# A recurrent branch and an attention without GpSimd arithmetic: products on VectorE, a value kept in DRAM, a first tap on ScalarE

## The chip, the cores and the metric

The kernel runs on one core of a Trainium2 chip. The engines of the core that matter here are TensorE (PE in the profile: matrix products), VectorE (DVE), ScalarE (ACT), GpSimd (POOL) and SyncE (SP, which here only issues DMAs). Each engine works through its own queue of instructions in a fixed order and waits on semaphores for the others. The metric is the time of one execution on the device in microseconds. Lower is better.

## What is computed

Two blocks in sequence on a tensor of 1024 positions by 1024 channels, all in float32. The change touches the recurrent branch of the first block, the tail of that block's MLP, and the row sums of the second block's attention. Of the reference:

```python
# first block
z = jnp.einsum("bsd,de->bse", rms_norm(x, g_mix), w_in) + b_in
va, ga, xb, gb, sa, sb = jnp.split(z, cuts, axis=-1)
u = causal_depthwise_conv(va * sigmoid(ga), conv_a_w, conv_a_b)      # 31 taps, 1024 channels
y_a = silu(layer_norm(u, ln_g, ln_b)) @ w_a_out
v = causal_depthwise_conv(xb, conv_b_w, conv_b_b)                    # 4 taps, 1536 channels
# rg_lru, 16 heads of 96 channels:
r = sigmoid(block_diag_linear(v, w_a, b_a)); i = sigmoid(block_diag_linear(v, w_x, b_x))
log_a = -8.0 * r * softplus(-lam); a = exp(log_a)
mult = sqrt(-expm1(2.0 * log_a)), with 1.0 at the first position
h = scan over positions of  h = a * h + mult * i * v
y_b = (h * gelu(gb)) @ w_b_out
x = x + (sigmoid(sa) * y_a + sigmoid(sb) * y_b) @ w_o
x = x + square(relu(rms_norm(x, g_mlp) @ w_1)) @ w_2
x = rms_norm(x, g_final)
# second block (mLSTM, pooling and memory attention branches)
s = einsum(q, k) * exp(dmat - m_t)        # causal, per chunk in the reference
h = (... + s @ v) / max(abs(... + sum(s, axis=-1)), exp(-m_t))
```

## The kernel before, in words

Every tensor lies with 128 channels in the partitions and positions along the free axis, in two halves of 512 positions (`hf`). A float32 matrix product is made as three products of split values (a high part made by a ScalarE copy, a low part made by a VectorE subtraction). A tile of 128 channels by 512 positions takes 24 matmuls (`ct`, `mm3`, L124 and L127). A weight block of 128x1024 arrives by DMA (L106, two buffers `wst`), gets its high part on ACT (L108) and its low part on DVE (L110).

The Tile scheduler places the instructions of all these code pieces into the engines' queues by priority at build time. After that the order of each queue is fixed.

The input projection of the first block, `mixer_in`, runs from about 20 to 690 us in four rounds `r` of `branch_b`. In a round:

- `branch_b_in` runs three times, for three blocks of 128 channels: two `ct` tiles, ACT moves them out to page `x6` with a bias (L376), POOL makes the first of the four short taps into page `x7` (L381, 128x1024), DVE adds the three others (L383), SP stores rows 96 to 127 to `v_d` (L385), and ACT and DVE split the result into `vh` and `vl`.
- a filler: in rounds 0 to 2 two more channel blocks of the long convolution, whose 31 taps are DVE instructions of 128x512 (L358) with low priority, spread over the following work; in round 3 tiles of the two sigmoid gates (`sig_chunk`, L471).
- four heads `n`. In each, ACT moves four gate tiles out of PSUM with a sigmoid (L416, into buffers `a`), then makes two exponentials (L421, two more buffers `a`), two tanh (L425) and two squares (L428, buffers `c`); DVE combines them (L429); ACT takes two roots (L432); DVE writes the start value (L433). For n < 3 PE makes the gelu input, two `ct` tiles, and ACT makes gelu (L442 for 96 rows into buffer `b`, L443 for the other 32 into `gl_d`). Then per half: POOL rebuilds the conv result r = vh + vl into a buffer `c` (L451, n < 3; the fourth head's r is `v_d`), POOL makes i * r (L454), DVE multiplies by the root (L455), DVE scans (L456), POOL multiplies by gelu (L458), SP stores the result to `p` (L460, L463).

There are six buffers `a`, and a head takes six. So the gates and exponentials of a head go into buffers that the head before has to have finished with. The last readers there are L455, L456 and, for the buffers of the two input gates, POOL's L458. There are five buffers `c`, of which `gl_d` holds two for the round. PSUM has four buffers `pa` (gates) and four `pm` (`ct`).

Elsewhere POOL makes half of the sums of squares at the end of the MLP (`square_sum`, L155, 14 additions of 128x512), and in the second block's attention (`mlstm_attn`) the causal select L789 and the running row sum L798 (40 additions). In the attention DVE makes the decay argument (L785), ACT its exponential (L786), DVE the product with the scores (L791), ACT and DVE split that (L131, L132), and PE's L800 and L801 use the split.

The lines of the last steps of a head, in before:

```python
                if n < 3:
                    G.tensor_tensor(r, src[hf][0].bitcast(F32), src[hf][1].bitcast(F32), ALU.add)
                else:
                    r = v_d[hf][rows, :]
                G.tensor_tensor(i_, i_, r, ALU.mult)
                V.tensor_tensor(i_, i_, m[hf][rows, :], ALU.mult)
                V.tensor_tensor_scan(i_, a[hf][rows, :], i_, 0.0 if prev is None else prev[:, HALF - 1:HALF], ALU.mult, ALU.add)
                prev = i_
                G.tensor_tensor(gt, gt, i_, ALU.mult)
```

## Time and profile before

| | us |
|---|---|
| median of 3 runs (2460.03 to 2460.41) | 2460.33 |
| the profiled execution | 2459.31 |
| its span, first to last instruction | 2457.6 |
| PE busy | 2366.8 (96%) |
| DVE busy | 1521.3 (62%) |
| ACT busy | 869.6 (35%) |
| POOL busy | 323.1 (13%) |
| mean granted clock of PE, share of full | 0.984 |

PE is busy nearly all the time, and the shares of the others are averages over stages that differ: DVE is at nine tenths or more in most slices of the first 740 us, and at three to six tenths in most of the rest. What the time depends on must be read by stretches: the row of 40 slices shows where an engine is full, the windows view gives the busy time, the instruction counts and PE's clock in a stretch, the view of waits tells which instruction ended PE's idle times, and the timeline of an engine shows what stood in its queue.

### The profile page before, as it was taken

How to read it: one execution, taken by the hardware profiler on the slowest of the kernel's cores; microseconds unless marked ns; L12 is line 12 of the kernel's file. 1: busy time of each engine (PE TensorE's matmuls, PEld its weight loads, DVE VectorE, ACT ScalarE, POOL GpSimd, SP SyncE). 2: the span in 40 equal slices, each digit the busy share in tenths (PEclk: the TensorE clock that was granted, in tenths of full speed). 3: DMA queues.
4: the chain of work that ended last, by engine and by line, in shares of the span. 5: the costliest groups of instructions: out<-in, count | busy, mean ns of one | idle time of the engine just before them, and what ended most of it. 6: DMA issues, size and time to landing. Idle time of an engine off the chain costs nothing.

```text
span 2457.6 us, 27022 instructions
## 1 busy us (share of the span) xinstructions
PE 2366.8 (96%) x10656; PEld 1946.1 (79%) x10656; DVE 1521.3 (62%) x2115; ACT 869.6 (35%) x1358; POOL 323.1 (13%) x198
## 2 busy tenths in 40 slices
PE   8996989989999999999999999999899999999998
PEld 6875867868878888888888888888688787777777
DVE  8998999698473424563333333434846557874766
ACT  6344254353652302342122112213524344442432
POOL 0127142153400000000000000001200002220110
PEclk9998999989999999999999999999999999999999
DMA  4111212113233422321211111121331111213331
GB/s 150 58 50 46 67 48 92 56 45 91 83 124 110 160 85 82 99 67 43 61 35 60 43 52 52 35 66 38 103 103 54 55 61 50 72 60 117 115 100 69
DMA packets 71104, 181.64 MB, mean 74 GB/s; under 512 B 8496, under 2 KB 11056, under 8 KB 70976
## 3 DMA queue, kind: packets, MB, share of 16 engines
q1 hardware_dynamic: 70976, 179.92, 23.4%
q8 instruction: 83, 1.36, 0.2%
q14 instruction: 45, 0.37, 0.0%
HBM read 148.92 MB, written 29.39 MB: 73 GB/s over the span
## 4 chain that ended last, share of the span: by engine, by line
PE 65%; DVE 22%; issue 5%; ACT 4%; POOL 3%; DMA 1%; SPq 0%; DVEq 0%; ACTq 0%; POOLq 0%
PE pm L124 41%; PE pm L127 20%; DVE e L358 8%; DVE wl L110 2%; DVE x L383 1%; POOL x L381 1%; DVE a L456 1%; DVE a L132 1%; PE pa L124 1%; DVE roll L723 1%; ACT wh L108 1%; PE pm L119 1%; DVE a L791 1%; DVE a L455 1%; DMA ld<-y 1%
## 5 line engine op out<-in xcount | busy, mean ns | idle before, releaser
L124 PE MATMUL pm<-acth,wl 128*128 128x512 f32 (+1 forms) x2480 | 968.0, 391 | 26.3 <-ACT c L443 13.2
L124 PE MATMUL pm<-actl,wh 128*128 128x512 f32 (+1 forms) x2480 | 966.6, 391 | 0.0
L127 PE MATMUL pm<-acth,wh 128*128 128x512 f32 (+1 forms) x2480 | 619.8, 387 | 0.0
L124 PEld LDWEIGHTS pm<-acth,wl 128*128 128x128 f32 x2480 | 471.7, 190 | 124.8 <-ACT c L443 14.5
L124 PEld LDWEIGHTS pm<-actl,wh 128*128 128x128 f32 x2480 | 471.6, 190 | 96.3 <-issue 0.7
L127 PEld LDWEIGHTS pm<-acth,wh 128*128 128x128 f32 x2480 | 461.4, 188 | 94.3 <-issue 1.2
L108 ACT ACTIVATE wh<-wst 128x1024 fp32r<-128x1024 f32 x209 | 219.9, 1055 | 544.9 <-PE pm L127 501.7
L110 DVE TENSOR_TENSOR wl<-wst,wh 128x1024 fp32r<-128x1024 f32 x209 | 257.7, 1235 | 94.7 <-ACT wh L108 94.4
L124 PE MATMUL pm<-e,wl 128*128 128x512 f32 x592 | 230.4, 389 | 0.0
L124 PE MATMUL pm<-e,wh 128*128 128x512 f32 x592 | 230.3, 389 | 0.0
L646 DVE TENSOR_TENSOR x<-pm,x 128x512 f32<-128x512 f32 x128 | 88.4, 691 | 180.1 <-PE pm L127 180.1
L155 POOL TENSOR_TENSOR row<-row,c 128x512 f32<-128x512 f32 x14 | 22.4, 1598 | 1057.9 <-ACT c L152 1057.5
L127 PE MATMUL pm<-e,wh 128*128 128x512 f32 x592 | 158.1, 389 | 0.0
L636 DVE TENSOR_TENSOR b<-b 128x512 f32<-128x512 f32 x64 | 44.3, 692 | 178.0 <-ACT b L634 178.0
L358 DVE SCALAR_TENSOR_TENSOR e<-roll,pv,e 128x507 f32<-128x507 f32 (+13 forms) x174 | 151.7, 927 | 0.0
L124 PEld LDWEIGHTS pm<-e,wl 128*128 128x128 f32 x592 | 111.1, 188 | 23.4 <-DVE wl L110 0.4
L124 PEld LDWEIGHTS pm<-e,wh 128*128 128x128 f32 x592 | 111.1, 188 | 23.1
L127 PEld LDWEIGHTS pm<-e,wh 128*128 128x128 f32 x592 | 111.1, 188 | 23.1
L634 ACT ACTIVATE b<-pm 128x512 f32<-128x512 f32 x64 | 38.3, 598 | 204.0 <-PE pm L127 203.2
L458 POOL TENSOR_TENSOR b<-b,a 96x512 f32<-96x512 f32 x24 | 73.7, 3090 | 76.9 <-DVE a L456 55.9
L798 POOL TENSOR_TENSOR a<-a,a 128x256 f32<-128x256 f32 (+2 forms) x40 | 59.0, 1474 | 102.5 <-DVE a L791 100.9
L789 POOL TENSOR_SCALAR_AFFINE_SELECT a<-a 128x128 f32<-128x128 f32 (+1 forms) x32 | 17.2, 537 | 408.9 <-ACT a L786 408.9
(315 smaller groups left out, 2557.7 us busy)
## 6 DMA issues: line engine op xcount, KB each, us to landing
wst<-in_w_in SPq DMA_DIRECT2D x89, 512.0 KB, 3.6
wst<-in_w SPq DMA_DIRECT2D x64, 512.0 KB, 3.5
sig<-b SPq DMA_DIRECT2D x32, 256.0 KB, 2.5
ld<-sig SPq DMA_DIRECT2D x32, 256.0 KB, 2.7
a<-p SPq DMA_DIRECT2D x24, 256.0 KB, 4.1
wst<-in_w_b_out SPq DMA_DIRECT2D x12, 512.0 KB, 4.3
y<-b SPq DMA_DIRECT2D x24, 256.0 KB, 2.0
ld<-y SPq DMA_DIRECT2D x24, 256.0 KB, 2.6
```

What stands on the lines that cost most here:

```text
L108: nc.scalar.activation(h, st, AF.Copy)
L110: nc.vector.tensor_tensor(l, st, h.bitcast(F32), ALU.subtract)
L119: self.nc.tensor.matmul(ps, a, b, start=i == 0, stop=i == n - 1)
L124: self.nc.tensor.matmul(ps, a, b, start=i == 0, stop=i == n - 1)
L127: self.nc.tensor.matmul(ps, aH, bH, start=i == 0, stop=i == n - 1)
L132: self.nc.vector.tensor_tensor(L, srcap, H.bitcast(F32), ALU.subtract)
L358: ops.append(lambda k=k: V.scalar_tensor_tensor(out[:, k:], x[:, :HALF - k], taps[k], out[:, k:], ALU.mult, ALU.add))
L458: G.tensor_tensor(gt, gt, i_, ALU.mult)
L634: A.activation(t, ps, AF.Relu)
L636: V.tensor_tensor(t2, t, t, ALU.mult)
L646: V.tensor_tensor(x, ps, x, ALU.add)
L798: G.tensor_tensor(acc[:, n0:], acc[:, n0:], e[:, n0:], ALU.add)
```

## The change

The four parts of the change:

1. `branch_b_in`: the first short tap L381 (12 instructions of 128x1024) goes from POOL to ACT, as an activation with scale and bias. Rows 0 to 95 of the conv result are also stored to a DRAM tensor `v` (24 stores of 96x512).
2. `branch_b`: r is no longer rebuilt on POOL; 24 DMAs load it from `v` into a buffer `c`, on SP's queue. The product i * r (32 instructions) and the product with gelu (32) go from POOL to DVE.
3. `mlp`: the 14 additions of L155 go from POOL to DVE.
4. `mlstm_attn`: the 40 additions of the row sum go from POOL to DVE.

POOL keeps the causal select and a few instructions at the end. After the change a new line stands in `branch_b_in` at L386, so that L416 becomes L417, L421 L422, L428 L429, L429 L430, L432 L433 and L433 L434. The load of r is L453, the product i * r L456, the product with the root L457, the scan L458, the product with gelu L460, its store L462; in the attention L785 becomes L787, L791 L793, L798 L800.

```diff
--- before.py
+++ after.py
@@ -378,11 +378,12 @@
 
         def wt(s):
             return self.vec("conv_b_w", c * 4 + 3 - s)
-        nc.gpsimd.tensor_scalar(v, xb, wt(0), self.vec("conv_b_b", c), ALU.mult, ALU.add)
+        nc.scalar.activation(v, xb, AF.Identity, scale=wt(0), bias=self.vec("conv_b_b", c))
         for s in range(1, 4):
             V.scalar_tensor_tensor(v[:, s:], xb[:, :S - s], wt(s), v[:, s:], ALU.mult, ALU.add)
         for hf in range(2):
             nc.sync.dma_start(v_d[hf][32 * j:32 * j + 32, :], v[HEAD:P, hf * HALF:(hf + 1) * HALF])
+            nc.sync.dma_start(self.v_dram[c][hf], v[:HEAD, hf * HALF:(hf + 1) * HALF])
         vh = self.page(f"x{j}", F32R)
         vl = self.page(f"x{3 + j}", F32R)
         self.split(v, vh, vl)
@@ -446,16 +447,17 @@
                 gl = gl_d
             prev = None
             for hf in range(2):
-                r, i_, gt = (self.tmp('c')[rows, :] if n < 3 else None), gate[2 * hf + 1][rows, :], gl[hf][rows, :]
+                i_, gt = gate[2 * hf + 1][rows, :], gl[hf][rows, :]
                 if n < 3:
-                    G.tensor_tensor(r, src[hf][0].bitcast(F32), src[hf][1].bitcast(F32), ALU.add)
+                    r = self.tmp("c")[rows, :]
+                    nc.sync.dma_start(r, self.v_dram[3 * g + n][hf])
                 else:
                     r = v_d[hf][rows, :]
-                G.tensor_tensor(i_, i_, r, ALU.mult)
+                V.tensor_tensor(i_, i_, r, ALU.mult)
                 V.tensor_tensor(i_, i_, m[hf][rows, :], ALU.mult)
                 V.tensor_tensor_scan(i_, a[hf][rows, :], i_, 0.0 if prev is None else prev[:, HALF - 1:HALF], ALU.mult, ALU.add)
                 prev = i_
-                G.tensor_tensor(gt, gt, i_, ALU.mult)
+                V.tensor_tensor(gt, gt, i_, ALU.mult)
                 if n < 3:
                     nc.sync.dma_start(self.p_dram[3 * g + n][hf][0:HEAD, :], gt)
                 else:
@@ -646,7 +648,7 @@
                         V.tensor_tensor(x, ps, x, ALU.add)
                     if e == 7:
                         acc1 = self.square_sum(acc1, x)
-                        acc2 = self.square_sum(acc2, x, self.vec("g_final", c), nc.gpsimd)
+                        acc2 = self.square_sum(acc2, x, self.vec("g_final", c))
                 if e == 7:
                     V.scalar_tensor_tensor(acc2, acc1, EPS, acc2, ALU.mult, ALU.add)
                     rs = self.rsqrt(self.spread(acc2, self.mean_d), EPS * EPS)
@@ -795,7 +797,7 @@
                 if acc is None:
                     acc = e
                 else:
-                    G.tensor_tensor(acc[:, n0:], acc[:, n0:], e[:, n0:], ALU.add)
+                    V.tensor_tensor(acc[:, n0:], acc[:, n0:], e[:, n0:], ALU.add)
                 vH, vL = v(h, j)
                 M(num[:, n0:], vL, pH[:, n0:], start=j == 0, stop=False)
                 M(num[:, n0:], vH, pL[:, n0:], start=False, stop=False)
@@ -1051,6 +1053,7 @@
             def dt(n, i, shape):
                 return dram.tile(list(shape), F32, tag=f"{n}{i}", name=f"{n}{i}")
             self.p_dram = [[dt("p", 2 * c + hf, (P, HALF)) for hf in range(2)] for c in range(12)]
+            self.v_dram = [[dt("v", 2 * c + hf, (HEAD, HALF)) for hf in range(2)] for c in range(12)]
             self.sig_dram = [[dt("sig", 2 * c + hf, (P, HALF)) for hf in range(2)] for c in range(16)]
             self.y_dram = [[dt("y", 2 * c + hf, (P, HALF)) for hf in range(2)] for c in range(12)]
             self.x_dram = [[dt("xd", 2 * c + hf, (P, HALF)) for hf in range(2)] for c in range(8)]
```

**DVE's queue, round 0, the second head.** Before, from the head's two L429 on. The names are those of the program with running numbers: `a` a gate buffer, `c` a buffer of r or of a square, `e` and `roll` outputs and inputs of the long convolution.

```order
L429 SCALAR_TENSOR_TENSOR a_1607<-c_1633,a_1607 96x512
L429 SCALAR_TENSOR_TENSOR a_1619<-c_1636,a_1619 96x512
L358 SCALAR_TENSOR_TENSOR e_124_868<-roll_398,tap_sum,e_124_868 128x510
L358 SCALAR_TENSOR_TENSOR e_181_1422<-e_155_1133,pv,e_181_1422 128x511
L358 SCALAR_TENSOR_TENSOR e_180_1370<-e_154_1132,pv,e_180_1370 128x511
L433 MEMSET a_1607 96x1
L358 SCALAR_TENSOR_TENSOR e_123_816<-roll_329,tap_sum,e_123_816 128x509
L455 TENSOR_TENSOR a_1613<-a_1613,a_1607 96x512
L455 TENSOR_TENSOR a_1625<-a_1625,a_1619 96x512
L456 SCALAR_TENSOR_TENSOR a_1613<-a_1627,a_1613 96x512
L358 SCALAR_TENSOR_TENSOR e_124_868<-roll_398,tap_sum,e_124_868 128x509
L456 SCALAR_TENSOR_TENSOR a_1625<-a_1629,a_1613,a_1625 96x512
```

After, from the same place (L430 is what was L429):

```order
L430 SCALAR_TENSOR_TENSOR a_1637<-c_1663,a_1637 96x512
L430 SCALAR_TENSOR_TENSOR a_1649<-c_1666,a_1649 96x512
L110 TENSOR_TENSOR wl_1984<-wst_1980,wh_1982 128x1024
L456 TENSOR_TENSOR a_1643<-a_1643,c_1734 96x512
L434 MEMSET a_1637 96x1
L358 SCALAR_TENSOR_TENSOR e_124_892<-roll_422,tap_sum,e_124_892 128x510
L457 TENSOR_TENSOR a_1643<-a_1643,a_1637 96x512
L456 TENSOR_TENSOR a_1655<-a_1655,c_1741 96x512
L458 SCALAR_TENSOR_TENSOR a_1643<-a_1657,a_1643 96x512
L457 TENSOR_TENSOR a_1655<-a_1655,a_1649 96x512
L460 TENSOR_TENSOR b_1703<-b_1703,a_1643 96x512
L458 SCALAR_TENSOR_TENSOR a_1655<-a_1659,a_1643,a_1655 96x512
```

The two L456 and the first L460 now stand between the two L430 and the second scan, together with a weight's L110; of the five L358 that stood in this piece one is left there, the others are further back. The first product, which needs a loaded `c`, is the fourth row.

**SP's queue, the same place.** `wst` is a weight block, `p` the stored result, `v` the new DRAM tensor. Before:

```order
L106 DMA wst_1950<-in_w_in 128x1024
L460 DMA p_99<-b_1558 96x512
L106 DMA wst_2020<-in_w_in 128x1024
L460 DMA p_100<-b_1586 96x512
L460 DMA p_101<-b_1673 96x512
L460 DMA p_102<-b_1701 96x512
```

After:

```order
L106 DMA wst_1980<-in_w_in 128x1024
L453 DMA c_1619<-v_123 96x512
L453 DMA c_1626<-v_124 96x512
L106 DMA wst_2052<-in_w_in 128x1024
L462 DMA p_99<-b_1588 96x512
L462 DMA p_100<-b_1616 96x512
L453 DMA c_1734<-v_125 96x512
L453 DMA c_1741<-v_126 96x512
L106 DMA wst_2124<-in_w_in 128x1024
```

Each of these heads now has two loads of r ahead of a weight load and of two stores of `p`; the second load of a head writes the buffer `c` that the head's first L430 has read.

**DVE's queue, the end of the MLP, second half.** `row` are the two running sums of squares, L658 (after: L660) the scaling of the residual with the last norm, `wl` the low part of a weight of the second block. Before:

```order
L658 SCALAR_TENSOR_TENSOR x_1024_6992<-x_1024_6992,pv,row_11715 128x512
L110 TENSOR_TENSOR wl_12294<-wst_12290,wh_12292 128x1024
L155 TENSOR_TENSOR row_11958<-row_11958,c_12036 128x512
L658 SCALAR_TENSOR_TENSOR x_1028_7023<-x_1028_7023,pv,row_11715 128x512
L110 TENSOR_TENSOR wl_12327<-wst_12323,wh_12325 128x1024
L155 TENSOR_TENSOR row_11958<-row_11958,c_12056 128x512
L658 SCALAR_TENSOR_TENSOR x_1032_7055<-x_1032_7055,pv,row_11715 128x512
L155 TENSOR_TENSOR row_11958<-row_11958,c_12076 128x512
L658 SCALAR_TENSOR_TENSOR x_1036_7087<-x_1036_7087,pv,row_11715 128x512
L110 TENSOR_TENSOR wl_12333<-wst_12329,wh_12331 128x1024
```

After:

```order
L155 TENSOR_TENSOR row_12006<-row_12006,c_12064 128x512
L155 TENSOR_TENSOR row_12008<-row_12008,c_12067 128x512
L110 TENSOR_TENSOR wl_12342<-wst_12338,wh_12340 128x1024
L155 TENSOR_TENSOR row_12006<-row_12006,c_12084 128x512
L155 TENSOR_TENSOR row_12008<-row_12008,c_12087 128x512
L110 TENSOR_TENSOR wl_12375<-wst_12371,wh_12373 128x1024
L155 TENSOR_TENSOR row_12006<-row_12006,c_12104 128x512
L155 TENSOR_TENSOR row_12008<-row_12008,c_12107 128x512
L155 TENSOR_TENSOR row_12006<-row_12006,c_12124 128x512
L155 TENSOR_TENSOR row_12008<-row_12008,c_12127 128x512
L155 TENSOR_TENSOR row_12006<-row_12006,c_12144 128x512
L110 TENSOR_TENSOR wl_12381<-wst_12377,wh_12379 128x1024
```

The sums of the second accumulator stand in turn with those of the first, and no L658 (L660) stands between the weights' L110 there.

## Rows read from the trace of the kernel before

**Rows 1.** Page, part 2: busy tenths of 40 slices of 61.4 us, two engines.

```profile
DVE  8998999698473424563333333434846557874766
...
POOL 0127142153400000000000000001200002220110
```

**Rows 2.** Windows view: busy us (instructions) PE, PEld, DVE, ACT, POOL; clock; DMA; GB/s.

```profile
100.00:150.00 50.00, 50.00 (x222) 41.38 (x221) 49.05 (x68) 14.06 (x19) 4.93 (x2) 1.00 0.16 48
150.00:250.00 100.00, 78.28 (x310) 62.67 (x310) 87.54 (x108) 48.00 (x73) 60.87 (x22) 0.88 0.17 50
300.00:400.00 100.00, 87.74 (x350) 69.96 (x349) 99.73 (x116) 52.66 (x80) 41.04 (x21) 0.91 0.19 57
500.00:550.00 50.00, 41.39 (x162) 33.17 (x161) 48.48 (x50) 24.18 (x38) 29.74 (x15) 0.86 0.18 51
1700.00:1800.00 100.00, 88.71 (x406) 73.31 (x405) 81.23 (x111) 51.75 (x80) 22.36 (x14) 0.93 0.28 89
2000.00:2350.00 350.00, 338.71 (x1511) 270.46 (x1511) 246.73 (x357) 149.16 (x245) 75.48 (x71) 1.00 0.27 84
```

**Rows 3.** Waits of PE, 80 to 720 us: line, releaser; total, times, longest.

```profile
PE pa L124 <- ACT a L416: 18.3, 6, 5.2
PE pm L124 <- ACT c L443: 13.2, 3, 6.0
PE pm L124 <- ACT b L471: 11.0, 2, 10.4
```

**Rows 4.** Timeline of ACT, round 0: start, us, instruction, [idle before].

```profile
227.90 0.72 ACT L421 ACTIVATE a<-a,nsp 96x512 f32<-96x512 f32 x1 [8.58 <-POOL b L458]
...
239.88 1.26 ACT L376 ACTIVATE x<-pm,pv 128x512 f32<-128x512 f32 x2
```

**Rows 5.** Timeline of POOL, the same stretch.

```profile
191.94 13.11 POOL L458 TENSOR_TENSOR b<-b,a 96x512 f32<-96x512 f32 x2 [3.70 <-DVE a L456]
```

**Rows 6.** Timeline of DVE, the same stretch.

```profile
207.59 1.29 DVE L429 SCALAR_TENSOR_TENSOR a<-c,a 96x512 f32<-96x512 f32 x2 [4.93 <-ACT c L428]
...
213.99 1.28 DVE L455 TENSOR_TENSOR a<-a,a 96x512 f32<-96x512 f32 x2
215.20 1.21 DVE L456 TENSOR_TENSOR_SCAN a<-a,a 96x512 f32<-96x512 f32 x1
...
218.16 1.37 DVE L358 SCALAR_TENSOR_TENSOR e<-e,pv,e 128x506 f32<-128x506 f32 x2
...
231.62 1.29 DVE L429 SCALAR_TENSOR_TENSOR a<-c,a 96x512 f32<-96x512 f32 x2 [4.89 <-ACT c L428]
```

**Rows 7.** Lines L429, L455, L458: duration ns min/median/max, first and last start.

```profile
L429 DVE SCALAR_TENSOR_TENSOR a<-c,a x32: 675/680/690, 157.5 to 670.3; 96x512 f32<-96x512 f32 x32
...
L455 DVE TENSOR_TENSOR a<-a,a x32: 672/678/1755, 168.9 to 675.0; 96x512 f32<-96x512 f32 x32
...
L458 POOL TENSOR_TENSOR b<-b,a x24: 1260/2000/11860, 171.5 to 662.9; 96x512 f32<-96x512 f32 x24
```

**Rows 8.** Timeline of ACT, round 3, where no long convolution runs.

```profile
614.06 2.40 ACT L416 ACTIVATE a<-pa,pv 96x512 f32<-96x512 f32 x4
...
630.37 2.41 ACT L416 ACTIVATE a<-pa,pv 96x512 f32<-96x512 f32 x4 [1.31 <-issue]
```

**Rows 9.** DMA view: issues, KB each, median us from issue to landing.

```profile
a<-p SPq DMA_DIRECT2D x24, 256.0 KB, 4.1
...
p<-b SPq DMA_DIRECT2D x24, 192.0 KB, 2.1
```

**Rows 10.** Timeline of DVE, end of the MLP.

```profile
1759.43 2.30 DVE L110 TENSOR_TENSOR wl<-wst,wh 128x1024 fp32r<-128x1024 f32 x1
```

**Rows 11.** Waits of PE, 1700 to 1800 us.

```profile
PE pm L124 <- DVE wl L110: 10.4, 4, 4.0
```

**Rows 12.** Waits of PE, 2000 to 2360 us.

```profile
PE pa L801 <- DVE a L132: 7.0, 12, 0.9
```

**Rows 13.** Timeline of DVE, attention.

```profile
2336.35 2.37 DVE L132 TENSOR_TENSOR actl<-ld,acth 128x512 fp32r<-128x512 f32 x2
```

## The prediction

> **What bounds the kernel now.** I read four views in this order: the row of 40 slices (where is an engine full), the windows (what PE lost there), the waits of PE (what it lost it to), and the timelines of the engines it waited for.
>
> PE sets the time: it is busy 96% of the span. Undisturbed it issues 222 matmuls in 50 us, 0.2252 us each, at a granted clock of 1.00 [rows 2]. In three stretches it falls short. From 150 to 250 us 310 matmuls ran, worth 69.8 us, so 30.2 us were lost; from 300 to 400 us 350 ran, 21.2 lost; from 500 to 550 us 162 ran, 13.5 lost [rows 2]. Together 64.9 us, and these are the heads of rounds 0, 1 and 2. Some 42 of them are waits: for L416 18.3, L443 13.2 and L471 11.0 [rows 3]. All three are ACT taking results out of PSUM; the rest is mostly the lower clock of these stretches (0.88, 0.91, 0.86).
>
> ACT is late because it is itself held: L421 waited 8.58 us for POOL's L458 [rows 4], whose buffers it needs. L458 had its scan long before. The POOL row shows two of them taking 13.11 us, though an undisturbed one takes 1.26 (minimum) and the worst 11.86 [rows 5, 7]. In that time DVE ran pairs of L358 back to back [rows 6]. The reverse is there too: a DVE product L455 of 0.678 us (median) takes up to 1.755 [rows 7]. So the two engines hold each other up, and POOL, with a mean load of 13%, is the slowest link of each head. Behind it DVE goes idle: 4.93 and 4.89 us ahead of the next heads' L429 [rows 6]. That chain, L458 to L421 to L428 to L429 and round again, sets the period of a head: 157.5 to 231.62 us are three periods, 74.1 us, from the first L429 [rows 6, 7]. In round 3, where no long convolution runs, a period is 16.3 us (614.06 to 630.37), set by ACT's own work [rows 8].
>
> The Trainium skill (page "SBUF — State Buffer", section "Who interferes with whom") says that a two-input DVE instruction and GpSimd share a port pair, that whoever issues first holds it for the whole instruction, and that the other is blocked. The trace agrees on the blocking; but 13.11 us for two products is many DVE instructions long, so here POOL loses far more than the one turn that rule suggests.
>
> **Part 1, the products on DVE and the loaded r.** It removes from rounds 0 to 2 all three POOL steps of the 12 heads and adds two DVE products per half, so 48 DVE instructions of 96x512. A pair of such takes 1.21 us by the starts 213.99 and 215.20 [rows 6], so 0.605 each, 29 us in all. What decides is the new period of a head, now set by DVE or ACT. By the changed order, DVE has between the first L430 of heads 0 and 3 of round 0: 40 L358 at 0.69 (half of 1.37), 30 other instructions of 512 columns at 0.605, six scans at 1.21, three L110 at 1.2 (twice 512 columns) and memsets: 27.6 + 18.2 + 7.3 + 3.6 + 0.2 = 56.9 us, against 74.1 measured [rows 6]. That is 17.2 us, or 57% of the 30.2 us lost there. DVE at 19 us a period stays above ACT's 16.3 [rows 8], and above PE's 60 matmuls x 0.2252 = 13.5, so DVE is next in line. I carry the same 57% to the other two rounds: 0.57 x 64.9 = 37 us. Two things would move it: DVE will not run without gaps (1 us per period costs 9), and the clock lost after each stop comes partly back (from 150 to 250 us PE was busy 78.28 us for 69.8 us worth of matmuls, 8.5 us in one round [rows 2]). I let them cancel: **-37 us**, between -18 and -65. In round 3 nothing is gained, since ACT holds the period.
>
> Ten of round 0's L358 leave its heads (50 there before, 40 now), so 6.9 us of DVE work go to the stretch behind. Between rounds DVE has little room: 49.05 of 50 us busy from 100 to 150 us [rows 2]. PE has no stop there now.
>
> The loads of r are new waits on DVE, with the L358 queued behind. The first half has its buffer a head earlier. The second's is freed by the head's first L430, so it is issued then and must land before the second L456. By the changed order, L430, L110 and L456 come between (0.6 + 1.2 + 0.6), then the memset that waits for ACT's root, an L358 and an L457 (0.7 + 0.6). The root is ready 1.31 + 1.2 us or so behind the second L430. That makes some 4.5 us of cover. Loads and stores of such size take 2.1 (192 KB, `p` stored) to 4.1 us (256 KB, `p` loaded) from issue to landing [rows 9]. I take the middle, so **0**; each us beyond the cover costs 12. On SP's queue the loads stand ahead of a weight load and two stores; the second load waits for L430 and holds the weight load back by less than a head, and `wst` has two buffers. The 24 stores of `v` share SP with 24 existing small ones while PE has its `ct` tiles to do. I put them at 0; page `x7` becomes free some 2 us later, under 48 matmuls (10.8 us) per block.
>
> **Part 2, the first tap on ACT.** Twelve instructions of 128x1024. No row shows this form; two 512-wide activations with a bias (L376) took 1.26 us [rows 4], so 1.3 at most. ACT is busy 14.06 of 50 us in such a stretch [rows 2] and the consumer, DVE's L383, is hidden under PE's 48 matmuls: **0**, between -2 (POOL no longer stretches DVE there) and +2.
>
> **Part 3, the sums at the end of the MLP.** PE waited 10.4 us, four times, for L110 [rows 11], and one L110 there took 2.30 us [rows 10] where 1.2 is usual, beside POOL's sums. The 14 additions add 8.5 us to DVE (14 x 0.605), but in the new order no L658 stands between the L110. I take **-6**, between -12 (all waits and a little clock) and +2 (DVE later by what doesn't fit into its gaps; it was busy 81.23 of 100 us [rows 2]).
>
> **Part 4, row sums of the attention.** 40 additions of at most 0.605 us put 24 us onto DVE, which was busy 246.73 of 350 us; PE was busy 338.71 [rows 2]. Its main wait is for DVE's L132, 7.0 us in 12 [rows 12]. For it: L132 pairs of 2.37 us instead of 1.3 [rows 13] go, as POOL is quiet but for L789. Against it: an addition may stand ahead of an L132 that PE waits for. **-3**, between -8 and +6.
>
> **Sum.** 2459.3 (the profiled execution) - 37 - 6 - 3 = 2413.3. It lies 1.0 below the median of the runs, which I add: **2414 us**. A difference under 0.2%, about 5 us, can't be told from no change.
>
> **The rivals.**
>
> A, DVE becomes the bound of all of rounds 0 to 2, not only of the heads. For: from 300 to 400 us it was already busy 99.73 of 100 us [rows 2], so what PE lost there comes back only as far as DVE's work shrinks, and the 6.9 us of L358 moved out of round 0's heads land where it has 1 us free in 50. Against: much of that busy time is stretch that goes with POOL. Half the gain is left on the branch: 2459.3 - 18.5 - 6 - 3 + 1 = 2433.
>
> B, all PE stops of the three places vanish, if DVE's order lets ACT run freely: 64.9 + 10.4 + 7.0 = 82.3, so 2378. Against: 19 us of DVE per period against 13.5 of PE.
>
> C, slower: the second load of r lands late. It stands in SP's queue, and DVE is blocked with everything behind it in each of 12 heads. It needs no more than a landing beyond 4.5 us of cover to cost, and it turns the branch's 37 us into a loss from 4.5 + 37/12 = 7.6 us on. At 9 us: 12 x 4.5 = 54, so 2459.3 - 37 - 9 + 54 + 1 = 2468. Against: 4.1 us is the longest of its kind in the rows [rows 9].
>
> D, slower: DVE is so full that added work simply lengthens it, and L421 waits for the DVE product as long as for POOL's. Then the 29 us of products come on top: 2459.3 + 29 + 1 = 2489. For: nine tenths in nearly all of the first ten slices [rows 1]. Against: the 4.9 us idle times ahead of L429, and the stretch, which leave room for about as much [rows 6, 7].
> The Trainium skill (page "Perfetto Trace Analysis", section "Optimizing Scalar/DVE Operations") speaks for D: with a saturated DVE it may make sense to move work off it, to ScalarE or even GpSimd, and this change does the reverse. The same passage adds that GpSimd shares a port with DVE, so that such a move might not help; the rows of the stretched products bear out that half.
>
> E, gains and new waits cancel to within 5 us: 2460.
>
> **How the numbers follow.** Main case 0.60, A 0.20, B 0.06, C 0.07, D 0.03, E 0.04. The main case alone spans about 2400 to 2428. With A and the nearer ends of the unknown costs the range is 2392 to 2450; outside it remain B, C, D and E, 0.20. Faster by over 0.2%: 0.86; within: 0.04; slower: 0.10.
>
> **What would show it.** Right: in rounds 0 to 2 the L430 of successive heads come some 19 us apart, not 24; L422 no longer waits for a product, or briefly; L358 pairs and the products show no stretched durations; PE does over 340 matmuls in the 100 us from 150 us on, with a clock over 0.90. Wrong: waits of L456 for the DMA of r (C); DVE at 100% with PE waiting for L323 or L417 in between rounds (A, D). At the end of the MLP PE's wait for L110 should fall under 5 us, and in the attention the one for L132 should not rise above 10. If the products on DVE show stretches as before, POOL was not the cause, and the sum falls.

## The result: 2386.65 us, and the profile after

| | before | after |
|---|---|---|
| median of the runs, us | 2460.18 (2459.68 to 2460.41, 4 runs) | 2386.65 (2385.94 to 2389.02, 4 runs) |
| span of the profiled execution, us | 2457.6 | 2384.2 |
| POOL busy, us | 323.1 | 18.8 |
| DVE busy, us | 1521.3 | 1498.1 |
| mean granted clock of PE | 0.984 | 0.995 |

The ratio is 0.9703, 95% interval 0.9686 to 0.972: 73.5 us faster. The forecast was 2414 us with a range of 2392 to 2450. The sign was right, the size was not: the time lies 5 us under the range. DVE is busy for 23 us less than before although it has 118 instructions more.

Both kernels issue the same 10,656 matmuls, and the start times of the matmul of the same number can be compared. Up to the end of the recurrent rounds the changed kernel is 56.5 us ahead (25.6 from round 0, 20.2 from round 1, 10.6 from round 2), the end of the MLP adds 5.3, and the attention 11.2. The terms of the prediction for these places were 37, 6 and 3.

The page, part 2, of the changed kernel (answers [rows 1]):

```profile
DVE  8999998995664234743343333435937467775866
...
POOL 0000000000000000000000000000000000000000
```

GpSimd is gone from the row. VectorE is at eight or nine tenths in the first nine slices, where one had stood at six before. The windows view of after; the second row is the three head periods of round 0, the others answer [rows 2]. Columns: stretch, length, busy us (instructions) of PE, PEld, DVE, ACT, POOL, then clock, DMA share, GB/s:

```profile
100.00:150.00 50.00, 50.00 (x222) 41.38 (x221) 50.00 (x71) 17.22 (x23) 0.00 (x0) 1.00 0.26 78
153.20:208.10 54.90, 54.90 (x244) 45.33 (x243) 54.76 (x84) 36.17 (x56) 0.00 (x0) 1.00 0.23 69
150.00:250.00 100.00, 97.36 (x423) 80.07 (x422) 99.86 (x138) 56.88 (x83) 0.00 (x0) 0.98 0.29 86
250.00:350.00 100.00, 99.81 (x440) 82.16 (x439) 100.00 (x151) 54.37 (x82) 0.00 (x0) 1.00 0.24 72
450.00:550.00 100.00, 97.35 (x429) 80.18 (x429) 96.58 (x130) 52.96 (x76) 0.00 (x0) 1.00 0.35 108
```

The same three periods in the kernel before:

```profile
157.50:231.60 74.10, 58.35 (x231) 46.36 (x229) 64.29 (x79) 34.90 (x54) 52.83 (x19) 0.91 0.12 38
```

From 150 to 250 us 423 matmuls ran where 310 did. The three periods of round 0 shrank from 74.1 to 54.9 us, and in the new ones PE is busy without a gap: 244 matmuls x 0.2252 = 54.95 us. TensorE has no free time left in that period, and VectorE, busy 54.76 of 54.90 us, hardly any.

DVE's timeline in round 0 (start, us, instruction; answers [rows 6]):

```profile
174.50 1.28 DVE L430 SCALAR_TENSOR_TENSOR a<-c,a 96x512 f32<-96x512 f32 x2
175.70 1.22 DVE L110 TENSOR_TENSOR wl<-wst,wh 128x1024 fp32r<-128x1024 f32 x1
176.83 0.68 DVE L456 TENSOR_TENSOR a<-a,c 96x512 f32<-96x512 f32 x1
...
181.09 0.68 DVE L460 TENSOR_TENSOR b<-b,a 96x512 f32<-96x512 f32 x1
...
191.38 1.29 DVE L430 SCALAR_TENSOR_TENSOR a<-c,a 96x512 f32<-96x512 f32 x2
...
208.06 1.30 DVE L430 SCALAR_TENSOR_TENSOR a<-c,a 96x512 f32<-96x512 f32 x2
```

The heads' L430 come at 174.50, 191.38 and 208.06, with no idle time ahead of them, 16.7 to 16.9 us apart, where they were 24 us apart. PE's waits from 60 to 640 us (line, releaser; us in total, times, longest) are down to one line (answers [rows 3]):

```profile
PE pm L124 <- ACT b L473: 5.5, 3, 2.7
```

And the stretched durations are gone (ns min/median/max; answers [rows 7]):

```profile
L358 DVE SCALAR_TENSOR_TENSOR e<-roll,pv,e x174: 710/745/784, 75.4 to 490.9; 128x511 f32<-128x511 f32 x12, 128x510 f32<-128x510 f32 x12, 128x509 f32<-128x509 f32 x12, 128x508 f32<-128x508 f32 x12
```

```profile
L457 DVE TENSOR_TENSOR a<-a,a x32: 661/681/704, 164.0 to 621.4; 96x512 f32<-96x512 f32 x32
```

### The profile page after: what moved, and what is told of

Same layout as the page of the kernel before. It is cut to its first block, busy times and chain, and to the rows that moved or that the text cites. A ratio compares the mean times of both kernels' runs of the same rounds, so it can differ in the third digit from the quotient of the medians.

```text
span 2384.2 us, 26982 instructions
## 1 busy us (share of the span) xinstructions
PE 2341.8 (98%) x10656; PEld 1934.1 (81%) x10656; DVE 1498.1 (63%) x2233; ACT 883.9 (37%) x1370; POOL 18.8 (1%) x44
## 4 chain that ended last, share of the span: by engine, by line
PE 72%; DVE 9%; ACT 2%; issue 2%; DMA 1%; POOL 0%; DVEq 0%; ACTq 0%; POOLq 0%
PE pm L124 45%; PE pm L127 22%; PE pa L124 2%; DVE e L358 1%; DVE wl L110 1%; PE pa L127 1%; DMA ld<-y 1%; DVE actl L132 1%; DVE row L155 1%; ACT wh L108 0%; DVE c L194 0%; DVE x L1033 0%; ACT c L152 0%; PE pa L802 0%; PE pa L948 0%
## 5 line engine op out<-in xcount | busy, mean ns | idle before, releaser
L124 PEld LDWEIGHTS pm<-acth,wl 128*128 128x128 f32 x2480 | 466.7, 188 | 106.8 <-ACT b L473 6.8
L110 DVE TENSOR_TENSOR wl<-wst,wh 128x1024 fp32r<-128x1024 f32 x209 | 255.3, 1224 | 87.9 <-ACT wh L108 87.3
L358 DVE SCALAR_TENSOR_TENSOR e<-roll,pv,e 128x507 f32<-128x507 f32 (+14 forms) x174 | 120.5, 748 | 0.0
L358 DVE SCALAR_TENSOR_TENSOR e<-roll,tap_sum,e 128x511 f32<-128x511 f32 (+14 forms) x90 | 63.2, 746 | 0.0
L152 ACT ACTIVATE c<-x 128x512 f32<-128x512 f32 (+1 forms) x63 | 36.1, 580 | 70.5 <-DVE x L607 35.0
L155 DVE TENSOR_TENSOR row<-row,c 128x512 f32<-128x512 f32 (+1 forms) x77 | 48.2, 642 | 15.6 <-ACT c L152 15.5
L579 DVE TENSOR_TENSOR b<-pm,ld 128x512 f32<-128x512 f32 x16 | 11.0, 690 | 71.7 <-PE pm L127 71.7
```

The lines of the kernel that those rows point to most:

```text
L110: nc.vector.tensor_tensor(l, st, h.bitcast(F32), ALU.subtract)
L124: self.nc.tensor.matmul(ps, a, b, start=i == 0, stop=i == n - 1)
L152: nc.scalar.activation(sq, x, AF.Square, scale=scale)
L155: (eng or nc.vector).tensor_tensor(acc, acc, sq, ALU.add)
L358: ops.append(lambda k=k: V.scalar_tensor_tensor(out[:, k:], x[:, :HALF - k], taps[k], out[:, k:], ALU.mult, ALU.add))
L579: V.tensor_tensor(t, ps, sg, ALU.mult)
```

## The experiments

All times are medians of several runs. The kernel before was run beside each group, and what a variant saves against it is taken from its median there: 2458.74 us for the first four runs, 2458.16, 2458.96, 2458.47 and 2459.49 for the later groups. Differences from the changed kernel are those of the medians as they stand (2386.65 us, beside which the kernel before took 2460.18). The kernel before moved by 2 us from group to group, so such a difference holds to about 2 us.

### The places apart

Three kernels carry the change at one place each. The branch alone, which has all of the change but these two lines:

```diff
-                        acc2 = self.square_sum(acc2, x, self.vec("g_final", c))
+                        acc2 = self.square_sum(acc2, x, self.vec("g_final", c), nc.gpsimd)
...
-                    V.tensor_tensor(acc[:, n0:], acc[:, n0:], e[:, n0:], ALU.add)
+                    G.tensor_tensor(acc[:, n0:], acc[:, n0:], e[:, n0:], ALU.add)
```

> Only the recurrent branch is changed (parts 1 and 2); the sums of the MLP and of the attention stay on GpSimd. By matching the same matmuls in the two traces the whole change saved 56.5 us up to the layer norm, 5.3 at the end of the MLP and 11.2 in the attention. Theory, the places are independent: 2460 - 56.5 = 2404, give or take 2. Rival, the later places gain only because the branch changed what reaches them: 2387 to 2395. By the prediction's own term for the branch (-37): 2423.

Measured 2401.23 us, 57.5 less than before. Now the attention alone (the line of the row sum changed from `G` to `V` in the kernel before):

> Only the 40 row sums of the attention go to VectorE. Theory, POOL's sums stretched VectorE's splits there and PE's weight loads waited for these: 2460 - 11 = 2449, and the waits of weight loads L801 for L132 (15.4 us in 22 in the kernel before) nearly vanish. Rival, the prediction's view that the added 24 us of VectorE work eat most of it: 2457.

Measured 2448.47 us, 10.3 less. The waits of PE's weight loads (the row PEld; us in total, times, longest) in the kernel before, over the whole span, and in this one:

```profile
PEld pa L801 <- DVE a L132: 15.4, 22, 1.3
```

```profile
PEld pa L801 <- DVE a L132: 1.5, 6, 0.5
```

The prediction had taken PE's row, 7.0 us [rows 12]. The weight loads show 15.4 us for the same line, and they drop to 1.5; of PE's own 7.0 us nothing is left. The gain of 10.3 us lies between the two rows. DVE's splits in the attention, as groups (busy us, mean ns | idle time before), before and in the changed kernel:

```profile
L132 DVE TENSOR_TENSOR a<-a,a 128x512 fp32r<-128x512 f32 (+2 forms) x46 | 42.7, 928 | 11.3 <-ACT a L131 11.0
```

```profile
L132 DVE TENSOR_TENSOR a<-a,a 128x512 fp32r<-128x512 f32 (+2 forms) x48 | 27.8, 578 | 12.3 <-ACT a L131 11.8
```

The mean falls from 928 to 578 ns, 15 us in all for these splits. So the 40 additions (22.2 us in the run of the attention alone) were paid for in good part by splits that are no longer stretched, in an engine with some three tenths of its time free.

The sums at the end of the MLP alone:

> Only the 14 sums at the end of the MLP go to VectorE. Theory, independent places: 2460 - 5 = 2455. Rival, the place gained only because the rest of the order shifted: 2460.

Measured 2453.0 us, 5.7 less. The three add up to 57.5 + 10.3 + 5.7 = 73.5: the places are independent, and the sum is the whole change. In the MLP, PE's wait for L110 fell from 10.4 us [rows 11] to 3.2, but a new one stands beside it, for a split that is now queued behind the sums:

```profile
PE pm L124 <- DVE e L132: 4.6, 1, 4.6
PE pm L124 <- DVE wl L110: 3.2, 3, 1.7
```

The two together are only 2.6 us less than the old wait. Part of the rest is TensorE's clock, which falls less: 0.95 of full from 1700 to 1800 us, where it was 0.93.

### One GpSimd step at a time

From the kernel before, only the last product of a head is moved:

```diff
-                G.tensor_tensor(gt, gt, i_, ALU.mult)
+                V.tensor_tensor(gt, gt, i_, ALU.mult)
```

> From the kernel before, only the last product of each head (with gelu, L458) goes to VectorE, 32 instructions; GpSimd still rebuilds r and makes i * r, and all else stays. Theory, the starved L458 that holds the gate buffers is what cost the time in the heads: most of the 56.5 us come, at least 40, so 2420 or less, and L421 no longer waits. Rival, all three GpSimd steps of a head cost alike: about a third, 19 us, 2441.

Measured 2439.2 us, 19.5 less, and 15.2 up to the end of the rounds. The size is the rival's, but the reason is not that the steps cost alike. POOL's timeline in round 0:

```profile
178.29 8.94 POOL L454 TENSOR_TENSOR a<-a,c 96x512 f32<-96x512 f32 x1 [2.00 <-ACT a L416]
...
213.91 13.41 POOL L454 TENSOR_TENSOR a<-a,ld 96x512 f32<-96x512 f32 x2 [15.11 <-ACT a L416]
```

i * r (L454), which had taken 1.62 us (median) and 2.79 at most, now takes 8.94 and 11.72. What DVE did in the time of the second one (the pairs of L358 between the rows shown are like the first):

```profile
215.54 1.39 DVE L358 SCALAR_TENSOR_TENSOR e<-roll,tap_sum,e 128x505 f32<-128x505 f32 x2
...
220.78 1.39 DVE L358 SCALAR_TENSOR_TENSOR e<-roll,tap_sum,e 128x503 f32<-128x503 f32 x2
222.09 1.28 DVE L429 SCALAR_TENSOR_TENSOR a<-c,a 96x512 f32<-96x512 f32 x2
223.29 1.22 DVE L110 TENSOR_TENSOR wl<-wst,wh 128x1024 fp32r<-128x1024 f32 x1
224.43 1.74 DVE L358 SCALAR_TENSOR_TENSOR e<-e,pv,e 128x504 f32<-128x504 f32 x1
```

The pairs take 1.39 us, as if GpSimd were not there, and when L454 ends at 225.63 one L358 is stretched to 1.74. The starvation (a GpSimd instruction held for as long as VectorE runs without a gap) moved to the next GpSimd step that meets a run of L358. L421, whose waits for L458 were the head of the chain, now waits 3.1 us in 4 for it; the loss came back through L455, which needs L454 (ScalarE's L416 waited 12.7 us for L455).

The other way round, r and i * r on VectorE, the last product left on GpSimd:

```diff
-                    G.tensor_tensor(r, src[hf][0].bitcast(F32), src[hf][1].bitcast(F32), ALU.add)
+                    V.tensor_tensor(r, src[hf][0].bitcast(F32), src[hf][1].bitcast(F32), ALU.add)
...
-                G.tensor_tensor(i_, i_, r, ALU.mult)
+                V.tensor_tensor(i_, i_, r, ALU.mult)
```

> From the kernel before: the rebuilt r and the product i * r (56 instructions) go to VectorE, GpSimd keeps only the product with gelu (L458). With the gelu product alone on VectorE, 15 us came in the heads, and the starved step became GpSimd's i * r (up to 11.72 us). Theory, one GpSimd step left in the chain of a head is enough to be starved by VectorE's runs of L358: L458 still takes up to 12 us, L421 waits for it, and the gain is under 20 us, so 2440 or more. Rival, each GpSimd step costs by its own length: two thirds of 56, so 2422.

Measured 2433.11 us, 25.0 less, between the two. L458 is still starved, as the theory said. The row is that of the fourth heads; in the others L458 takes up to 8.86 us, where it had taken 11.86 [rows 7]:

```profile
L458 POOL TENSOR_TENSOR c<-c,a x8: 1291/2730/10694, 225.3 to 654.9; 96x512 f32<-96x512 f32 x8
```

The rounds gain 15.2 us with the one step moved and 28.0 with the other two, 43.2 together. With all three moved and only the first tap left on GpSimd it is 51.0 (the run under "The first tap"), and 56.5 with the tap moved too. So 7 to 8 us come only when no GpSimd step is left in the chain.

### GpSimd busy, and nobody waiting

Is it enough that GpSimd works, without any engine waiting for it? The changed kernel, with idle products:

```diff
+    def pool_load(self, gt):
+        nc = self.nc
+        p = self.smalls.tile([P, 1], F32, tag="pace", name=self.name("pace"))
+        nc.vector.tensor_copy(p[0:HEAD, :], gt[:, 0:1])
+        nc.gpsimd.tensor_copy(self.scr[0:HEAD, 0:1], p[0:HEAD, :])
+        for i in range(3):
+            nc.gpsimd.tensor_tensor(self.scr[0:HEAD, :], self.pv[0:HEAD, 0:448], self.pv[0:HEAD, 0:448], ALU.mult)
...
                 V.tensor_tensor(gt, gt, i_, ALU.mult)
+                self.pool_load(gt)
```

> The changed kernel, and beside it idle work on GpSimd: after each half of a head three products of 96x448 from a constant into a scratch tile that nobody reads, released by a copy of one column on VectorE (96 products in all, 72 in rounds 0 to 2). Nobody waits for them. Theory, the two engines hold each other up by being busy at the same time: VectorE's instructions beside them are stretched again (half a stretch of 0.9 us per GpSimd instruction as before: 33 us in rounds 0 to 2, of which 10 to 33 reach the time), 2397 to 2420, and GpSimd's products beside runs of L358 take up to 10 us and more. Rival, only the waits of the chain for GpSimd mattered, not that it was busy: 2387 to 2389.

Measured 2429.24 us: 42.6 us more than without, above the theory's 2420, far from the rival. VectorE's waits show none for GpSimd up to 700 us. This is the cost of contention by itself, for work that nobody uses; the 32 added copies on VectorE, 4.3 us in all, are in it. DVE's timeline, with the idle products beside it:

```profile
183.12 1.95 DVE L458 TENSOR_TENSOR_SCAN a<-a,a 96x512 f32<-96x512 f32 x1
...
193.34 1.42 DVE L358 SCALAR_TENSOR_TENSOR e<-e,pv,e 128x511 f32<-128x511 f32 x1
194.69 0.73 DVE L358 SCALAR_TENSOR_TENSOR e<-roll,tap_sum,e 128x508 f32<-128x508 f32 x1
195.34 1.41 DVE L358 SCALAR_TENSOR_TENSOR e<-e,pv,e 128x510 f32<-128x510 f32 x1
```

A scan that takes 1.22 us takes 1.95, an L358 1.42 instead of 0.73. In all DVE's instructions were stretched by 55 us (each against the shortest of its kind, 80 of them, all beside a GpSimd instruction); in the rounds DVE has hardly any free time, so most of that reached the end. By the same count 62 instructions were stretched by 64 us in the kernel before, up to 700 us, all beside a GpSimd instruction, and none in the changed kernel. The other direction, GpSimd's products (ns min/median/max), and the windows of the longest one and of round 0's heads:

```profile
L474 POOL TENSOR_TENSOR scr<-pv x96: 929/1262/23959, 180.0 to 678.6; 96x448 bf16<-96x448 f32 x96
```

```profile
391.40:415.30 23.90, 23.90 (x108) 19.77 (x107) 23.90 (x33) 8.06 (x10) 23.90 (x1) 1.00 0.30 100
150.00:250.00 100.00, 92.03 (x392) 74.60 (x392) 99.89 (x128) 52.70 (x78) 60.78 (x32) 0.97 0.28 80
```

One product of under 1.3 us lasted 23.96 us. In its stretch DVE was busy 23.90 of 23.90 us in 33 instructions, without a gap.

The Trainium skill (page "SBUF — State Buffer", section "Who interferes with whom") has it that the holder of the shared ports blocks the other for one whole instruction. Blocking in both directions is what the rows show; but GpSimd's turn did not come after one DVE instruction: it waited through 33 here, and through some 15 in the kernel before (the first of the two products of 13.11 us [rows 5]).

### What r over DRAM is worth

The changed kernel with r rebuilt on GpSimd, no store and no load:

```diff
-            nc.sync.dma_start(self.v_dram[c][hf], v[:HEAD, hf * HALF:(hf + 1) * HALF])
...
-                    nc.sync.dma_start(r, self.v_dram[3 * g + n][hf])
+                    G.tensor_tensor(r, src[hf][0].bitcast(F32), src[hf][1].bitcast(F32), ALU.add)
```

> The changed kernel, but r is rebuilt on GpSimd as before (24 instructions), with no store to DRAM and no load. Theory, the rebuild is now the one GpSimd step in the chain and is starved beside the L358; VectorE's product waits for it: 2400 to 2425. Rival, the rebuild can be done early, since its inputs lie there for long, and VectorE never waits: 2387 to 2390, which would make the DRAM route needless.

Measured 2396.87 us: 10.2 over the changed kernel, just under the theory's range. The rebuild (L452 there; durations, and who waited for it) is stretched but not starved, and VectorE's product waits for it a little:

```profile
L452 POOL TENSOR_TENSOR c<-x,x x24: 1606/2258/3410, 89.8 to 607.8; 96x512 f32<-96x512 f32 x24
...
  DVE a L455: 8.3, 7
```

The same with the addition on VectorE:

```diff
-                    G.tensor_tensor(r, src[hf][0].bitcast(F32), src[hf][1].bitcast(F32), ALU.add)
+                    V.tensor_tensor(r, src[hf][0].bitcast(F32), src[hf][1].bitcast(F32), ALU.add)
```

> The changed kernel, but r is rebuilt by an addition on VectorE (24 of 96x512) in place of the store to DRAM and the load. Theory, in the heads VectorE now needs as long as TensorE (54.9 us for three periods against 241 matmuls x 0.2252 = 54.3), so 18 additions x 0.605 = 10.9 us in rounds 0 to 2 show nearly in full: 2394 to 2398. Rival, the DRAM route is worth nothing, because other work can move: 2387.

A miss for both: 2379.13 us, **7.5 us under the changed kernel** (5.5 by what each saves against the kernel before in its own group). Eighteen more additions on a VectorE that seemed full cost nothing that shows, and the DRAM route costs. Against the run just before, of the same group, it is 17.7 us for nothing but the engine of the 24 additions. With the stores of v kept beside that addition, read by nobody:

> The variant that rebuilds r by an addition on VectorE (2379.1), and beside it the 24 stores of v to DRAM that nobody reads. The route over DRAM was slower by 7.5 us than the addition. Theory, the stores are not the cause but the place that the scheduler gives to the rounds' last sigmoid tiles (L473 behind the roots, PE stops of 3.0 us at 212 and 500 us in the changed kernel, 1.3 and none with the addition): 2379 to 2381. Rival, the stores hold page x7 and so the first tap on ScalarE (7.7 us of waits for them), and PE behind it: 2384 to 2388.

2380.31 us: the stores are free. What is left is the loads, or what they do to the order of the queues. The loads land 2.3/2.5/4.0 us after issue (min/median/max), and VectorE has no wait for them:

```profile
DMA to landing us min/median/max: 2.3/2.5/4.0
```

But the queues differ. The two traces, compared by matmuls of the same number, show where the addition is ahead in the rounds: 3.0 us at 212 us and 3.0 at 500 us, less 1.0 at 346 us. At 212 and 500 us the changed kernel has PE's two long stops for L473. The first, and ScalarE's timeline there:

```profile
PE pm L124 <- ACT b L473: 2.6, 1, 2.6
```

```profile
209.25 1.15 ACT L433 ACTIVATE a<-a 96x512 f32<-96x512 f32 x2 [1.31 <-DVE a L430]
211.72 0.69 ACT L473 ACTIVATE b<-pm,pv 128x512 f32<-128x512 f32 x1 [1.31 <-issue]
212.30 1.05 ACT L108 ACTIVATE wh<-wst 128x1024 fp32r<-128x1024 f32 x1
214.10 1.06 ACT L108 ACTIVATE wh<-wst 128x1024 fp32r<-128x1024 f32 x1 [0.75 <-DMA wst<-in_w_in]
215.07 0.68 ACT L473 ACTIVATE b<-pm,pv 128x512 f32<-128x512 f32 x1
```

PE's stop ended at 212.46 us, with the first of the two L473. That one stands behind the roots L433, which waited for VectorE's L430 of the fourth head. With the addition the order at this place is the same, but the fourth head's L429 comes at 206.1 us instead of 208.06, and PE stops for 0.9 us only. PE's waits for the line are 1.9 us instead of 5.5:

```profile
PE pm L124 <- ACT b L472: 1.9, 2, 1.0
```

The head is later with the loads because of VectorE's order: in round 0 nine L358 and an L110 stand between the first head's L430 and its first product, and with the addition six L358 and the two additions (beside three entries that both have), so that the product starts 9.7 us behind L430 and not 7.5. The first period is 21.3 us instead of 19.7.

To test what L473's place costs, the sigmoid of `sig_chunk` gets the gelu's priority, first everywhere. (The expectation takes the second L473 behind the two weight copies for the one that PE stopped for; the rows above show that it was the first, behind the roots.)

```diff
-            nc.scalar.activation(t, ps, AF.Sigmoid, bias=self.vec("b_in", 40 + c))
+            with self.urgent():
+                nc.scalar.activation(t, ps, AF.Sigmoid, bias=self.vec("b_in", 40 + c))
```

> The changed kernel with one priority changed: the sigmoid that takes the tiles of sig_chunk out of PSUM (L473) gets the urgent priority that the gelu has. In round 0 of the changed kernel the second L473 stood behind two weight copies L108, the second of which waited for its DMA, and PE stopped 3.0 us for it; in the variants without loads of r one L108 stands between. Theory, this place in ScalarE's queue is what the loads of r cost: PE's waits for L473 (5.5 us in 3) shrink and the time falls to 2379 to 2383. Rival, the loads themselves cost (their DMAs, or the waits for them): 2386 or more.

> The variant with r by an addition on VectorE (2379.1), with the same urgent priority for the sigmoid of sig_chunk. Its PE waits for that line are 1.9 us in 2, so theory: 2375 to 2379. Rival, the urgent sigmoids delay the chain of the last head (roots, weight copies) by as much: 2379 to 2384.

Both worse, 2391.22 and 2386.31 us. The matched matmuls say why: against the same kernels without the priority the rounds gain 1.5 and 1.3 us, and the layer norm behind them, which has such tiles too, loses 10.0 and 8.7. So the pair told nothing on the loads, and it was repeated with the priority in the rounds alone:

```diff
+            with self.urgent() if c < 12 else nullcontext():
+                nc.scalar.activation(t, ps, AF.Sigmoid, bias=self.vec("b_in", 40 + c))
```

> The changed kernel with the urgent priority for the sigmoid of sig_chunk in the rounds alone (chunks 0 to 11), not in the layer norm behind them. With the priority everywhere the trace had gained 1.5 us more than the changed kernel up to the end of the rounds (4.4 in round 0) and lost 9.6 in the layer norm. Theory, the place of L473 in ScalarE's queue is a part of what the loads of r cost: 2384 to 2386. Rival, the place is worth nothing over all rounds: 2387 or more.

> The variant with r by an addition on VectorE, with the urgent priority in the rounds alone. With the priority everywhere its rounds had gained 1.3 us and its layer norm lost 7.3. Theory: 2377 to 2378.5, under the variant without it (2379.1). Rival, the priority moves the loss elsewhere: 2380 or more. If the loads of r cost only through L473's place, this one and the one with loads come within 2 us of each other.

2380.15 us (2375.53 to 2382.11) with the loads, under the theory's 2384, and 2377.47 (2376.01 to 2378.1) with the addition, as forecast. PE has no wait for the sigmoid left in the rounds of either. The gap between the two ways to get r shrinks from 7.5 (or 5.5) to 2.7 us. So half or more of what the DRAM route costs is PE's stops for the rounds' last sigmoids, as the places of the stops in the traces say too. That the loads make the scheduler place VectorE's products later is read from the order alone; no run tests it. What the other 2.7 us are stays open, and they are within the scatter of these runs. The variant with the addition and the priority has the lowest median of the study, at 0.967 of before (0.9654 to 0.9686). Without the priority VectorE's plain addition is better than the change's DRAM route by more than the scatter, with it no difference is shown.

### The first tap

The changed kernel, with L381 left on GpSimd:

```diff
-        nc.scalar.activation(v, xb, AF.Identity, scale=wt(0), bias=self.vec("conv_b_b", c))
+        nc.gpsimd.tensor_scalar(v, xb, wt(0), self.vec("conv_b_b", c), ALU.mult, ALU.add)
```

> The changed kernel, but the first short tap (L381, 12 instructions of 128x1024) stays on GpSimd. Theory, VectorE is now full between the heads' products (50.00 of 50 us busy from 100 to 150 us), so a GpSimd tap is starved there and VectorE's next taps wait for it or are stretched: 12 times 1 us of stretch or more where VectorE sets the pace, 2392 to 2410. Rival, the prediction's term of 0 for this part, since TensorE's tiles cover it: 2385 to 2389.

Measured 2392.11 us, 5.5 more, at the theory's lower end. The tap's durations, and the wait for it:

```profile
L381 POOL TENSOR_SCALAR x<-x,pv x12: 1584/2830/6036, 80.5 to 543.3; 128x1024 f32<-128x1024 f32 x12
...
  DVE x L383: 11.5, 11
```

On ScalarE the same tap takes 1.25 us:

```profile
L381 ACT ACTIVATE x<-x,pv x12: 1239/1248/1252, 80.8 to 536.3; 128x1024 f32<-128x1024 f32 x12
```

## Why the prediction missed, step by step

**What bounds the kernel, and why: right in the contention, too narrow in the chain.** L458 was starved beside the runs of L358 and held L421 and with it the heads; with GpSimd out of the chain the waits of PE for L416 and L443 are gone. But L458 was not the whole of it: moved alone, it gave 15.2 us in the rounds. That contention costs time without any wait for GpSimd's result is shown by the idle products: 42.6 us for work with no reader. How the 56.5 us divide between stretched VectorE instructions and waits for GpSimd no run separates.

**The head's new period: right in VectorE's work.** Forecast 56.9 us for round 0's three periods, measured 54.9. VectorE ran without the gaps I had allowed for (1 us a period).

**The step that failed: from the period to the branch, 37 us instead of 56.5.** I divided the 17.2 us by which three periods shrink by the 30.2 us that PE lost from 150 to 250 us, and carried the 57% to the other rounds. The 17.2 us came: up to the last matmul ahead of PE's longest stop (at 226.82 us in the kernel before) the changed kernel is 17.2 us ahead. But the 30.2 also held what the fourth head lost by the same L421, behind the third period: that stop, PE's 10.4 us wait for L471, the longest entry there [rows 3]. Behind it the changed kernel is 25.0 us ahead, and 25.6 when the clock is back. The gain was 25.6 of the 30.2 in round 0, 20.2 of 21.2 in round 1, 10.6 of 13.5 in round 2, or 87% of the 64.9. Nor did the 57% carry over: by the starts of L429 and L430 the three periods shrank by 14.9 us in round 1 and 13.7 in round 2.

A second error did not enter the 37 us, but the chances. I put PE's floor at 60 matmuls, 13.5 us a head, from the head's own tiles. PE had 244 in three periods, 18.3 us each, because other tiles run between them. VectorE's 18.3 us a head were therefore no new bound: PE needs as long. A period must be compared with all that an engine does in it, which the windows view would have told: 231 matmuls in the old three periods.

**The attention: 3 instead of 11.2.** Two terms failed. The wait was taken from PE's row for L132 (7.0 us) and not from that of its weight loads (15.4), for the same line. And the 24 us of additions, for which the forecast left only 3 of the 7.0, cost nothing that shows.

**The end of the MLP: right in size**, 6 forecast, 5.3 to 5.7 measured. The wait for L110 fell as forecast, to 3.2 us; the new wait of 4.6 us for a split behind the sums was not foreseen.

**The loads of r: the wait right, the zero wrong.** Landing 2.5 us (median), 4.0 at most, under the 4.5 us of cover; rival C did not come. The stores cost nothing. But with the loads other entries stand at other places in the queues, and that costs 5 to 7 us, half of it or more in PE's stops for L473. The prediction looked for a cost in transfers and waits, and only at the places where its terms rested.

**The first tap: 0 put, 5.5 found** when it is left behind, outside the bounds of -2 to +2. It was worth more because by then VectorE had no time left between the heads (50.00 of 50 us from 100 to 150 us), so that a GpSimd instruction there hurts; the term was costed in the old surroundings.

**The rivals.** A asked what VectorE's fullness would hold back. VectorE was indeed at 100 of 100 us in round 1, and PE lost almost nothing, since a large part of the old busy time was stretch (64 us in the rounds). B, all PE stops gone (2378), was nearest, at a chance of 0.06. It was priced too low because of PE's floor. D, where the added products simply lengthen a full VectorE, is refuted; its row of slices also shows nine tenths in six of the first ten [rows 1], not in nearly all.

The Trainium skill (page "Perfetto Trace Analysis", section "Optimizing Scalar/DVE Operations") says that with a saturated DVE it may make sense to move work off it, even to GpSimd, and that the shared port may spoil this. Here work moved onto a saturated VectorE made it less busy, by 23 us over the span: the second half of the passage decides.

## What to carry to other kernels

Where GpSimd and VectorE work in the same stretch, count the stretch of VectorE's instructions and the length of GpSimd's as one cost: elementwise work on GpSimd can be dearer than the same work on a full VectorE. Move all GpSimd steps of a chain if any, since one that is left is still starved, and the parts were worth less than their sum. And when a wait goes, compare the next engine's period with everything that TensorE does in that time, and read the weight loads' waits beside the matmuls'.

## What the runs showed of the hardware that was not expected

A GpSimd product of under 1.3 us can be held for 23.96 us beside VectorE running without a gap, and even a copy of one column for 18.82 us (POOL's timeline of the kernel with the idle products):

```profile
548.33 18.82 POOL L472 CAST scr<-pace 96x1 bf16<-96x1 f32 x1 [3.78 <-DVE pace L471]
```

It is no matter of one instruction's turn. Idle GpSimd work that nobody waits for cost this kernel 42.6 us, some four fifths of the time by which it stretched VectorE's instructions up to 700 us (54 us).
